# One unit of ten products per head pair, and a new order of the stages, in a two-layer decoder trunk

## The chip, the cores and the metric

The kernel runs on one core of a Trainium2 chip. The metric is the time of one execution in microseconds (us), as the device reports it. Engine names: PE is the tensor engine (matmuls), DVE the vector engine, ACT the scalar engine, POOL the GpSimd engine, SP the engine whose queue issues all the transfers (DMAs) here.

## The reference

The trunk has two residual layers over 256 positions of width 1024, in float32. Each layer normalizes its input, projects it once, runs two mixers, multiplies every mixer's output by a gate, and projects the result back. Layer 0 has a depthwise convolution and an attention over blocks (called b in the kernel). Layer 1 has an attention with three branches (c) and a sliding-window attention (d). The part that is changed is the end of the three branches:

```
kc = _rmsnorm(_compress(k_cmp, ...), kn_cmp)          # compressed keys, by a small MLP
vc = _compress(v_cmp, ...)
p_c = _masked_softmax(s_c, dist_c >= 0)
o_cmp = einsum(p_c, vc)                               # compressed branch
o_slc = ... einsum(p, selected v)                     # selected branch
o_win = _banded_attention(qg, k_win, v_win, ...)      # local branch
o = gt[0] * o_cmp + gt[1] * o_slc + gt[2] * o_win     # gates, per head and position
```

Eight query heads share two key heads, so they are worked on as four pairs.

## The kernel before, in words

Everything is computed transposed, with channels or positions on the 128 partitions. A projection is made of three float32r matmuls per piece (high by high, low by high, high by low): the weight is loaded as `raw_X`, ACT makes its high part `hi_X`, DVE or POOL the rest `lo_X`, and the input stands ready as `hhi` and `hlo`. The loads go through a ring of five `raw` buffers, the parts through nine.

The names in the rows: `pj_X` is a projection's accumulator (`kv`, `cc`, `qc`, `kd`, `qd`, `zc`, `zd` in layer 1); `ps_ht` holds transposes of the normalized input of layer 1, from which `hhi` and `hlo` come; `po` is the output projection, whose result DVE adds to `x`; `xc` is the input of the compressing MLP, of which POOL makes a part from `kv` and a part from `sw`, a copy of `kv` that a DMA has moved to other partitions; `ps_hid` is that MLP's first product, 64 matmuls on small tiles; `ps_sc` and `st` belong to the compressed branch's softmax.

An attention of a head pair goes: scores on PE (`s_c`), scores plus bias and their maximum on DVE (`sn`, `mn_c`), exponentials on ACT (`p_c`), a reciprocal on DVE (`r_c`), four scalings on POOL (`p_c<-p_c,r_c`), six transposes on PE (`pt_c`), two copies on ACT (`a_c`), the products with the values on PE (`po_c`), and the gate on DVE (`y_c`). Its stages are called `attc jb` (to the exponentials) and `pvc jb` (the rest), for pair j and branch b (0 selected, 1 local); the last attention has `attd j` and `pvd j`.

The order is not that of the code. A `Recorder` takes every instruction down, each with the stage in which it stands, and its `issue()` places them one after the other: among those that its own estimate of costs lets start, the stage that stands first in the table `ORDER` wins. It also decides whether DVE or POOL makes a `lo` part. All instructions go out through one call in `issue()`, so all rows of the profile carry its line, L384, and only the names tell them apart. Matmuls that stand under `nc.together()` are one unit: nothing is placed between them. In the kernel before, `pv()` makes such a unit of four products for each branch, and the local branch's unit has the compressed branch's two products in it as well:

```
with nc.together():
    for e in range(2): ... matmul(po[o, :S], v(0, e), a0[:, e, :], start=first, stop=False)
    for e in range(2): ... matmul(po[o, P:S], v(1, e), a1[:, e, :], start=False, stop=last)
    if more:
        for e in range(2): ... matmul(po[o, :S], *more(e), start=False, stop=True)
```

The profile counts each of these float32 products as two matmuls, so the units stand in its rows as `po_c x8` and `po_c x12`.

Of the kernel before, what the change touches and what calls it, by code (L numbers as in the profile page):

```python
# [13 lines left out]
P = 128  # L14
S = 256
# [4 lines left out]
HD = 64  # L20
# [374 lines left out]
def _landing(bus, t, nbytes):  # L395

    t = max(bus, t + 1300.0)
    for until, rate in RATES:
# [14 lines left out]
               POOL=dict(PE=135.0, ACT=100.0, DVE=60.0, POOL=96.0, SP=100.0),  # L413
               SP=dict(PE=250.0, ACT=100.0, DVE=100.0, POOL=100.0, SP=100.0))
EXTRA = dict(copy=(0.0, 20000.0), minus=(80.8, 0.0), scale=(0.0, 20000.0, 20000.0))
ORDER = ["attc 11", "attb 0", "w kv 0", "za 3", "uv", "w uv 1", "pvd 0", "w zd 1", "o1 10", "pvc 31", "pvc 11",
# [11 lines left out]
RAWS, PARTS = 5, 9  # L428
WARM = 7
SHIFT = 8  # L430
# [6 lines left out]
def tile_trunk(ctx: ExitStack, tc: tile.TileContext, i: dict, out: bass.AP):  # L437
    ctx.enter_context(tc.manual_schedule())
    nc = Recorder(tc.nc, tc)
# [8 lines left out]
    def bank(tag, bufs, name):  # L448
        return psum.tile([P, 512], F32, tag=tag, bufs=bufs, name=name)
# [296 lines left out]
        nc.copy(a1, t1[:, :2 * P].rearrange("p (e t) -> p e t", e=2))  # L746
        return a0, a1

    def pv(po, a0, a1, v, first, last, more=None):

        with nc.together():
            for e in range(2):
                o = slice(e * HD, (e + 1) * HD)
                nc.tensor.matmul(po[o, :S], v(0, e), a0[:, e, :], start=first, stop=False)
            for e in range(2):
                o = slice(e * HD, (e + 1) * HD)
                nc.tensor.matmul(po[o, P:S], v(1, e), a1[:, e, :], start=False, stop=last)
            if more:
                for e in range(2):
                    o = slice(e * HD, (e + 1) * HD)  # L760
                    nc.tensor.matmul(po[o, :S], *more(e), start=False, stop=True)
# [11 lines left out]
    w = load_w("ug", [cols_of(0, 512, 512)])  # L773
# [23 lines left out]
    w = load_w("uv", [cols_of(0, 0, 512)])  # L797
# [19 lines left out]
    w = load_w("qb", [cols_of(0, 1536, 512)])  # L817
# [3 lines left out]
    w = load_w("kb", [cols_of(0, 2048, 512)])  # L821
# [43 lines left out]
    for j in range(4):  # L865
        nc.stage(f"attb {j}")
        pt = bank("pt", 2, f"ps_qk{j}")
        for b in range(NB):
            nc.tensor.transpose(pt[:, b * P:(b + 1) * P], qn[b][:, j * P:(j + 1) * P], ident)
            nc.tensor.transpose(pt[:, S + b * P:S + (b + 1) * P], kn[b][:, j * P:(j + 1) * P], ident)  # L870
        qk = work.tile([P, 2, S], F32, tag="qk", name=f"qk{j}")
        qT, kT = qk[:, 0], qk[:, 1]
        nc.scaled(qT, pt[:, :S], q8["b_qnorm_g"][:, j:j + 1])
        nc.scaled(kT, pt[:, S:], col("b_knorm_g"))
        mn, den, pp = pair_softmax(f"b{j}", j, qT, kT, False, none_init)
        nc.stage(f"pvb {j}")
        r = work.tile([P, 4], F32, tag="r", bufs=4, name=f"r_b{j}")
        nc.vector.reciprocal(out=r, in_=den)
        for u in range(4):
            scale_p(pp[u // 2][:, u % 2, :], r[:, u:u + 1])  # L880
        a0, a1 = transposed(pp[0], pp[1], f"b{j}")
        po = bank("pt", 2, f"po_b{j}")
        pv(po, a0, a1, lambda kb, e: v0[:, kb, (2 * j + e) * HD:(2 * j + e + 1) * HD], True, True)
        gate_y(4 + j, po, z[:, 4 + j], f"b{j}")

    nc.stage("ln")
# [245 lines left out]
    for j in range(4):  # L1132
        g = j // 2
        po = bank("o", 1, f"po_c{j}")
        for br in range(2):
            nc.stage(f"attc {j}{br}")
            mn, den, pp = pair_softmax(f"c{j}{br}", j, qTn[:, j], kTn[:, g, br], False, none_init)
# [5 lines left out]
            for u in range(4):  # L1143
                scale_p(pp[u // 2][:, u % 2, :], r[:, u:u + 1])
            a0, a1 = transposed(pp[0], pp[1], f"c{j}{br}")
            pv(po, a0, a1, lambda kb, e: keep[:, 2 * kb + br, P + g * HD:P + (g + 1) * HD], br == 0, False,
               (lambda e: (vcb[:, 2 * j + e, :], ac)) if br else None)
        gate_y(j, po, z1[:, j], f"c{j}")

    for j in range(4):  # L1150
# [12 lines left out]
            scale_p(pp[u // 2][:, u % 2, :], r[:, u:u + 1])  # L1163
        a0, a1 = transposed(pp[0], pp[1], f"d{j}")
        po = bank("o", 1, f"po_d{j}")
        pv(po, a0, a1, lambda kb, e: vd[:, kb, P + g * HD:P + (g + 1) * HD], True, True)
        gate_y(4 + j, po, z1[:, 4 + j], f"d{j}")

    wo = [load_w(f"o1{n}", [i["w_out"][1][:, n * 512:(n + 1) * 512]]) for n in range(2)]
# [103 lines left out]
```

## Time and profile before

| | us |
|---|---|
| median of 3 runs (269.99 to 270.39) | 270.2 |
| profiled execution | 270.53 |
| its span (first to last instruction) | 268.5 |
| PE busy | 260.0 (97%) |
| DVE busy | 197.1 (73%) |
| ACT busy | 172.3 (64%) |
| POOL busy | 108.0 (40%) |

The profiled execution is 0.33 us above the median. Busy times are sums over instructions; matmuls overlap each other, so the share of PE says that PE is seldom without an instruction, and not how fast it works. The rest of the profile is read by its steps: which instruction followed which, at what distance, and what ended an idle time.

### The profile page before, as it was taken

The numbers are of one execution on the slowest core, as the hardware profiler recorded it, in microseconds if no ns is written. First come the engines' busy times: TensorE is split into PE (matmuls) and PEld (weight loads), VectorE is DVE, ScalarE is ACT, GpSimd is POOL, SyncE is SP. The second block draws the span as 40 slices with busy tenths as digits, with TensorE's granted clock in tenths as the row PEclk, the third lists the DMA queues.
The fourth block names the chain that finished last, engine by engine and source line by source line (L and its number), as shares of the span: only waits on it lengthen the run. The fifth ranks groups of instructions, "written<-read, shape, count | busy, mean of one in ns | idle before, by whom it ended". The sixth has DMA issues, their size and how long they took to land.

```text
span 268.5 us, 5004 instructions
## 1 busy us (share of the span) xinstructions
PE 260.0 (97%) x1693; PEld 212.4 (79%) x1693; DVE 197.1 (73%) x511; ACT 172.3 (64%) x458; POOL 108.0 (40%) x143
## 2 busy tenths in 40 slices
PE   7889999999999999999899999999999999999994
PEld 5679987878789988878679879678878987667684
DVE  1399999999999999458987213589979856765231
ACT  2267779799995656656467223688869768775300
POOL 0100019858735923202424474154991420545000
PEclk9999999999999999999999999999999999999999
DMA  6998987725763445301858827498885200000031
GB/s 198 361 386 286 354 279 279 212 101 160 236 193 121 171 147 145 89 0 40 282 158 221 231 67 250 160 343 254 273 289 149 86 4 0 2 0 1 2 117 39
DMA packets 28072, 44.89 MB, mean 167 GB/s; under 512 B 3344, under 2 KB 10256, under 8 KB 28048
## 3 DMA queue, kind: packets, MB, share of 16 engines
q1 hardware_dynamic: 28048, 44.58, 50.9%
q8 instruction: 13, 0.21, 0.3%
q14 instruction: 11, 0.09, 0.1%
HBM read 43.26 MB, written 1.05 MB: 165 GB/s over the span
## 4 chain that ended last, share of the span: by engine, by line
PE 61%; DVE 13%; DMA 12%; ACT 5%; POOL 3%; issue 3%; SPq 2%; DVEq 0%; POOLq 0%; ACTq 0%
PE po L384 15%; PE pj_zd L384 5%; PE pj_vb L384 4%; PE pj_za L384 4%; PE pj_zb L384 4%; PE pj_qc L384 4%; PE pj_kv L384 4%; DMA h<-in_prm_dram 3%; PE po_c L384 3%; DMA raw_o<-in_w_out_dram 3%; DMA raw_qd<-in_o_w_in_dram 2%; SPq L384 2%; DMA raw_kb<-in_e_w_in_dram 2%; PE pj_cc L384 2%; PE pt_c L384 2%
## 5 line engine op out<-in xcount | busy, mean ns | idle before, releaser
L384 POOL TENSOR_SCALAR p_c<-p_c,r_c 128x128 f32<-128x128 f32 (+1 forms) x32 | 19.5, 625 | 27.1 <-ACT th_zd L384 8.9
L384 DVE SCALAR_TENSOR_TENSOR acc_m<-hc,cw,acc_m 128x256 f32<-128x256 f32 x58 | 28.0, 483 | 0.2
L384 DVE SCALAR_TENSOR_TENSOR acc_o<-hc,cw,acc_o 128x256 f32<-128x256 f32 x58 | 28.1, 484 | 0.0
L384 PE MATMUL po<-hi_o,yh 128*128 128x512 f32 (+1 forms) x72 | 27.0, 382 | 0.0
L384 PE MATMUL po<-hi_o,yl 128*128 128x512 f32 (+1 forms) x72 | 27.0, 379 | 0.0
L384 PE MATMUL po<-lo_o,yh 128*128 128x512 f32 (+1 forms) x72 | 26.8, 374 | 0.0
L384 POOL TENSOR_TENSOR lo_vb<-raw_vb,hi_vb 128x1024 fp32r<-128x1024 f32 x4 | 9.5, 2409 | 25.7 <-ACT hi_vb L384 25.7
L384 ACT CAST hi_o<-raw_o 128x1024 fp32r<-128x1024 f32 x16 | 16.4, 1045 | 3.4 <-DMA raw_o<-in_w_out_dram 1.6
L384 DVE TENSOR_TENSOR lo_o<-raw_o,hi_o 128x1024 fp32r<-128x1024 f32 x13 | 15.7, 1213 | 1.5 <-ACT hi_o L384 1.5
L384 PE MATMUL pj_ug<-h,raw_ug 128*128 128x256 f32 x64 | 15.4, 392 | 1.4 <-DMA raw_ug<-in_e_w_in_dram 1.4
L384 PEld LDWEIGHTS po<-hi_o,yl 128*128 128x128 f32 x72 | 13.5, 188 | 2.9 <-issue 0.7
L384 ACT ACTIVATE p_c<-sn,mn_c 128x256 f32<-128x256 f32 (+1 forms) x32 | 14.3, 450 | 2.2 <-DVE mn_c L384 2.2
L384 PEld LDWEIGHTS po<-hi_o,yh 128*128 128x128 f32 x72 | 13.6, 189 | 2.7 <-issue 0.3
L384 PEld LDWEIGHTS pj_ug<-h,raw_ug 128*128 128x128 f32 x64 | 12.2, 197 | 3.8 <-issue 2.3
L384 PEld LDWEIGHTS po<-lo_o,yh 128*128 128x128 f32 x72 | 13.6, 188 | 1.9
L384 POOL TENSOR_TENSOR rsx<-ssx,mhalf 128x1 f32<-128x1 f32 x4 | 2.7, 680 | 27.0 <-DVE ssx L384 27.0
L384 DVE TENSOR_TENSOR x<-x,po 128x512 f32<-128x512 f32 (+1 forms) x9 | 5.6, 625 | 8.6 <-PE po L384 8.6
L384 DVE CUSTOM_DVE_ANT_0 sn<-s_c,shp 128x256 f32<-128x256 f32 (+1 forms) x32 | 10.7, 349 | 1.6 <-ACT p_c L384 0.9
L384 POOL TENSOR_TENSOR lo_o<-raw_o,hi_o 128x1024 fp32r<-128x1024 f32 x3 | 7.2, 2417 | 7.0 <-ACT hi_o L384 7.0
L384 PE MATMUL pj_zd<-hlo,hi_zd 128*128 128x256 f32 x32 | 9.4, 295 | 0.0
L384 POOL TENSOR_SCALAR p_b<-p_b,r_b 128x128 f32<-128x128 f32 (+1 forms) x16 | 8.6, 555 | 1.9 <-DVE r_b L384 1.5
L384 PE MATMUL pj_zc<-hhi,lo_zc 128*128 128x256 f32 x32 | 9.2, 287 | 0.2 <-DVE lo_zc L384 0.2
(334 smaller groups left out, 916.5 us busy)
## 6 DMA issues: line engine op xcount, KB each, us to landing
raw_o<-in_w_out_dram SPq DMA_DIRECT2D x16, 512.0 KB, 5.1
raw_uv<-in_e_w_in_dram SPq DMA_DIRECT2D x4, 512.0 KB, 8.3
raw_qb<-in_e_w_in_dram SPq DMA_DIRECT2D x4, 512.0 KB, 5.4
raw_kb<-in_e_w_in_dram SPq DMA_DIRECT2D x4, 512.0 KB, 5.8
raw_vb<-in_e_w_in_dram SPq DMA_DIRECT2D x4, 512.0 KB, 4.7
raw_zb<-in_e_w_in_dram SPq DMA_DIRECT2D x4, 512.0 KB, 4.5
raw_za<-in_e_w_in_dram SPq DMA_DIRECT2D x4, 512.0 KB, 3.6
raw_kv<-in_o_w_in_dram SPq DMA_DIRECT2D x4, 512.0 KB, 3.7
```

The lines of the kernel that those rows point to most:

```text
L384: getattr(self.real[e], method)(*args, **kw)
```

## The change

`pv()` takes a list of branches and puts all their products, and the compressed ones, under one `nc.together()`. For the three branches this makes one unit of ten products per head pair, issued in the stage `pvc j1`; the callers for b and d only pass their one branch as a list. The table `ORDER` is written anew from end to end: its entries all stand in another order, so instructions move on every engine, from the first layer on. The work is the same: 1476 matmul instructions with the same shapes.

```diff
-ORDER = ["attc 11", "attb 0", "w kv 0", "za 3", "uv", "w uv 1", "pvd 0", "w zd 1", "o1 10", "pvc 31", "pvc 11",
...
+ORDER = ["pvb 2", "w zc 1", "kd 0", "norm0 r1", "za 1", "norm0 0", "o0 01", "ln", "pvd 1", "norm0 r0", "w qc 0",
...
-    def pv(po, a0, a1, v, first, last, more=None):
-
+    def pv(po, sides, more=None):
+
+
+        n = 0
         with nc.together():
-            for e in range(2):
-                o = slice(e * HD, (e + 1) * HD)
-                nc.tensor.matmul(po[o, :S], v(0, e), a0[:, e, :], start=first, stop=False)
-            for e in range(2):
-                o = slice(e * HD, (e + 1) * HD)
-                nc.tensor.matmul(po[o, P:S], v(1, e), a1[:, e, :], start=False, stop=last)
+            for a0, a1, v in sides:
+                n += 1
+                for e in range(2):
+                    o = slice(e * HD, (e + 1) * HD)
+                    nc.tensor.matmul(po[o, :S], v(0, e), a0[:, e, :], start=n == 1, stop=False)
+                for e in range(2):
+                    o = slice(e * HD, (e + 1) * HD)
+                    nc.tensor.matmul(po[o, P:S], v(1, e), a1[:, e, :], start=False, stop=n == len(sides) and not more)
             if more:
...
         po = bank("o", 1, f"po_c{j}")
+        sides = []
         for br in range(2):
...
-            pv(po, a0, a1, lambda kb, e: keep[:, 2 * kb + br, P + g * HD:P + (g + 1) * HD], br == 0, False,
-               (lambda e: (vcb[:, 2 * j + e, :], ac)) if br else None)
+            sides.append((a0, a1, lambda kb, e, br=br: keep[:, 2 * kb + br, P + g * HD:P + (g + 1) * HD]))
+        pv(po, sides, lambda e: (vcb[:, 2 * j + e, :], ac))
         gate_y(j, po, z1[:, j], f"c{j}")
```

**The unit itself.** On PE, the products of head pair 0 before (`a0_c00` and `a1_c00` are the selected branch, `a0_c01` and `a1_c01` the local one, `vcb` the compressed one; some hundred other instructions stand where the dots are):

```order
L384 MATMUL s_c201_117_2568<-kTn_20_1764,qTn_28_2020 128x256
L384 MATMUL po_c0_97_2573<-a0_c00_202_2217,keep_21_1684 64x256 x2
L384 MATMUL po_c0_97_2573<-a1_c00_203_2235,keep_21_1684 64x128 x2
L384 MATMUL pj_zd0_86_2584<-hhi_4_186,hi_zd0_113_2317 128x256
...
L384 MATMUL pj_zd3_89_2803<-hhi_4_186,hi_zd1_115_2347 128x256
L384 MATMUL po_c0_97_2573<-a0_c01_213_2509,keep_21_1684 64x256 x2
L384 MATMUL po_c0_97_2573<-a1_c01_214_2607,keep_21_1684 64x128 x2
L384 MATMUL po_c0_97_2573<-ac_185_2680,vcb_25_2215 64x256 x2
L384 MATMUL pj_zd3_89_2803<-hlo_5_199,hi_zd1_115_2347 128x256
```

And with the change:

```order
L384 MATMUL s_c111_112_2626<-kTn_20_1753,qTn_28_2181 128x256
L384 MATMUL po_c0_97_2636<-a0_c00_202_2591,keep_21_1684 64x256 x2
L384 MATMUL po_c0_97_2636<-a1_c00_203_2619,keep_21_1684 64x128 x2
L384 MATMUL po_c0_97_2636<-a0_c01_213_2568,keep_21_1684 64x256 x2
L384 MATMUL po_c0_97_2636<-a1_c01_214_2579,keep_21_1684 64x128 x2
L384 MATMUL po_c0_97_2636<-ac_185_2438,vcb_25_2169 64x256 x2
```

The two pieces of pair 0 stand as one; the same holds for pair 3, while the pieces of pairs 1 and 2 stood next to each other already.

**The start of layer 1.** On DVE, between the output projection of layer 0 and the first projection of layer 1, before (`x1` is the residual, `lo_kv` and `lo_cc` are weight parts, `hlo` the low part of the new input):

```order
L384 TENSOR_TENSOR lo_kv2_70_1562<-raw_kv2_35_1329,hi_kv2_69_1546 128x2x512
L384 TENSOR_TENSOR lo_kv3_72_1571<-raw_kv3_36_1369,hi_kv3_71_1559 128x2x512
L384 TENSOR_TENSOR x1_2_105<-x1_2_105,po010_57_1447 128x512
L384 SCALAR_TENSOR_TENSOR hlo_5_199<-ps_ht100_60_1543,hhi_4_186 128x4x128
L384 SCALAR_TENSOR_TENSOR hlo_5_199<-ps_ht101_61_1553,hhi_4_186 128x4x128
L384 TENSOR_TENSOR x1_2_105<-x1_2_105,po011_59_1341 128x512
```

And with the change:

```order
L384 TENSOR_TENSOR lo_kv2_70_1561<-raw_kv2_35_1376,hi_kv2_69_1544 128x2x512
L384 SCALAR_TENSOR_TENSOR hlo_5_194<-ps_ht100_60_1541,hhi_4_186 128x4x128
L384 SCALAR_TENSOR_TENSOR hlo_5_194<-ps_ht101_61_1548,hhi_4_186 128x4x128
L384 TENSOR_TENSOR lo_kv3_72_1584<-raw_kv3_36_1417,hi_kv3_71_1571 128x2x512
L384 TENSOR_TENSOR lo_cc0_74_1593<-raw_cc0_37_1447,hi_cc0_73_1581 128x2x256
L384 TENSOR_TENSOR lo_cc1_76_1600<-raw_cc1_38_1487,hi_cc1_75_1589 128x2x256
L384 TENSOR_TENSOR x1_2_105<-x1_2_105,po011_59_1439 128x512
```

`hlo` has moved ahead of one `lo_kv` and of an addition to `x1`, and `lo_cc0` and `lo_cc1`, which POOL made before, stand on DVE.

**The compressing MLP.** On PE, the first of its products before, behind the last matmuls of the query projection `pj_qc`:

```order
L384 MATMUL pj_qc0_70_1852<-hi_qc3_87_1722,hhi_4_186 128x512
L384 MATMUL pj_qc0_70_1852<-lo_qc3_88_1734,hhi_4_186 128x512
L384 MATMUL pj_qc0_70_1852<-hi_qc3_87_1722,hlo_5_199 128x512
L384 MATMUL ps_hid_76_1934<-w1k0_49_1759,xc_22_1331 32x256 x2
L384 MATMUL ps_hid_76_1934<-w1v0_50_1775,xc_22_1331 32x256 x2
```

And with the change:

```order
L384 MATMUL pj_qc0_70_1851<-hi_qc1_83_1694,hhi_4_186 128x512
L384 MATMUL pj_qc0_70_1851<-lo_qc1_84_1708,hhi_4_186 128x512
L384 MATMUL ps_hid_76_1919<-w1k0_49_1759,xc_22_1303 32x256 x2
...
L384 MATMUL ps_hid_76_1919<-w1v1_52_1859,xc_22_1303 32x256 x2
L384 MATMUL pj_qc0_70_1851<-hi_qc1_83_1694,hlo_5_194 128x512
L384 MATMUL pj_qc0_70_1851<-hi_qc2_85_1710,hhi_4_186 128x512
```

The first half of the MLP's products now stands 13 matmuls ahead of the end of `pj_qc0`; the second half, one block before, has become two.

## Rows read from the trace of the kernel before

**Rows 1.** Page: busy time by engine, then the shares of the chain that ended last.

```profile
PE 260.0 (97%) x1693; PEld 212.4 (79%) x1693; DVE 197.1 (73%) x511; ACT 172.3 (64%) x458; POOL 108.0 (40%) x143
PE 61%; DVE 13%; DMA 12%; ACT 5%; POOL 3%; issue 3%; SPq 2%; DVEq 0%; POOLq 0%; ACTq 0%
```

**Rows 2.** The chain that ended last, in order of time: start, us, engine and group.

```profile
204.31 0.80 PE po_c L384 x8
...
212.94 0.86 PE s_c L384 x8
...
218.83 1.23 PE po_c L384 x12
...
221.87 1.88 PE po_c L384 x20
```

**Rows 3.** Timeline of PE, into the unit at 218.76: start, us, engine, instruction.

```profile
218.43 0.28 PE L384 MATMUL pj_zd<-hhi,lo_zd 128*128 128x256 f32 x1
218.55 0.28 PE L384 MATMUL pj_zd<-hhi,hi_zd 128*128 128x256 f32 x1
218.76 0.87 PE L384 MATMUL po_c<-a_c,keep 128*64 128x256 f32 x8
```

**Rows 4.** Timeline, all engines, at layer 1's start (in brackets idle time and releaser).

```profile
124.16 4.59 DVE L384 TENSOR_TENSOR lo_kv<-raw_kv,hi_kv 128x1024 fp32r<-128x1024 f32 x3
...
126.25 3.65 POOL L384 TENSOR_TENSOR lo_cc<-raw_cc,hi_cc 128x512 fp32r<-128x512 f32 x2 [3.45 <-ACT hi_cc L384]
...
128.67 0.68 DVE L384 TENSOR_TENSOR x<-x,po 128x512 f32<-128x512 f32 x1
128.82 0.39 PE L384 MATMUL pj_kv<-lo_kv,hhi 128*128 128x512 f32 x1
129.27 1.28 DVE L384 SCALAR_TENSOR_TENSOR hlo<-ps_ht,hhi 128x512 fp32r<-128x512 f32 x2
...
130.00 0.50 PE L384 MATMUL pj_kv<-hi_kv,hlo 128*128 128x512 f32 x1 [0.80 <-DVE hlo L384]
...
130.34 0.40 PE L384 MATMUL pj_kv<-hi_kv,hhi 128*128 128x512 f32 x1
130.57 0.39 PE L384 MATMUL pj_kv<-lo_kv,hhi 128*128 128x512 f32 x1
```

**Rows 5.** Page: DVE's splits of 128x1024 (count, busy, mean ns, idle before).

```profile
L384 DVE TENSOR_TENSOR lo_o<-raw_o,hi_o 128x1024 fp32r<-128x1024 f32 x13 | 15.7, 1213 | 1.5 <-ACT hi_o L384 1.5
```

**Rows 6.** Timeline, all engines, around the MLP's input and its first products.

```profile
148.95 0.37 ACT L384 COPY kv<-pj_cc 128x256 f32<-128x256 f32 x1
...
154.69 3.45 POOL L384 TENSOR_TENSOR xc<-sw,prm 64x120 f32<-64x120 f32 x8 [3.25 <-DMA sw<-kv]
...
159.99 0.41 PE L384 MATMUL ps_hid<-w1k,xc 128*32 128x256 f32 x2
```

**Rows 7.** DMA issues, 146 to 162 us: KB each, median us to landing.

```profile
w1k<-in_c_k_w_dram SPq DMA_DIRECT2D x4, 256.0 KB, 4.2
...
sw<-kv SPq DMA_DIRECT2D x2, 128.0 KB, 4.3
```

**Rows 8.** Timeline of PE, two more waits.

```profile
189.20 0.28 PE L384 MATMUL pj_zc<-hlo,hi_zc 128*128 128x256 f32 x1
189.64 0.39 PE L384 MATMUL pj_zc<-hhi,lo_zc 128*128 128x256 f32 x1 [0.16 <-DVE lo_zc L384]
...
198.42 0.33 PE L384 MATMUL pt_c<-ident,p_c 128*128 128x128 f32 x1
199.30 0.33 PE L384 MATMUL ps_sc<-ident,st 128*128 128x128 f32 x1 [0.55 <-ACT st L384]
```

**Rows 9.** Timeline, DVE and POOL at once in layer 0.

```profile
63.36 0.48 DVE L384 SCALAR_TENSOR_TENSOR acc_m<-hc,cw,acc_m 128x256 f32<-128x256 f32 x1
63.43 2.41 POOL L384 TENSOR_TENSOR lo_zb<-raw_zb,hi_zb 128x1024 fp32r<-128x1024 f32 x1
63.75 0.48 DVE L384 SCALAR_TENSOR_TENSOR acc_o<-hc,cw,acc_o 128x256 f32<-128x256 f32 x1
```

**Rows 10.** Timeline of POOL: scalings of one head pair in layer 0, and in layer 1.

```profile
71.51 0.84 POOL L384 TENSOR_SCALAR p_b<-p_b,r_b 128x128 f32<-128x128 f32 x2 [0.42 <-PE s_b L384]
...
217.01 1.62 POOL L384 TENSOR_SCALAR p_c<-p_c,r_c 128x128 f32<-128x128 f32 x4 [3.26 <-DVE r_c L384]
```

More of the change, by code (lines that the diff above doesn't have):

```diff
@@ L882, in tile_trunk @@
         po = bank("pt", 2, f"po_b{j}")
-        pv(po, a0, a1, lambda kb, e: v0[:, kb, (2 * j + e) * HD:(2 * j + e + 1) * HD], True, True)
+        pv(po, [(a0, a1, lambda kb, e: v0[:, kb, (2 * j + e) * HD:(2 * j + e + 1) * HD])])
         gate_y(4 + j, po, z[:, 4 + j], f"b{j}")
@@ L1165, in tile_trunk @@
         po = bank("o", 1, f"po_d{j}")
-        pv(po, a0, a1, lambda kb, e: vd[:, kb, P + g * HD:P + (g + 1) * HD], True, True)
+        pv(po, [(a0, a1, lambda kb, e: vd[:, kb, P + g * HD:P + (g + 1) * HD])])
         gate_y(4 + j, po, z1[:, 4 + j], f"d{j}")
```

22 rows, old and new, of the table ORDER are left out of this document.

## The prediction, made before the changed kernel ran

> **What bounds the kernel now.** I read the busy times first, then the chain of work that ended last, then PE's timeline wherever two matmuls stand farther apart than their kind usually does. PE is busy 260.0 of 268.5 us and makes up 61% of the chain [rows 1], so the time is PE's list of instructions, plus the places where PE finds its next operand not ready. A change that does the same matmuls can gain in two ways only: cheaper neighbours on PE, or fewer waits. After the loads of the first 57 us I find these waits that are worth anything: 0.95 us at the start of layer 1 [rows 4], 0.3 us at 189.6 and 0.76 us at 199.3 [rows 8]; some others are 0.1 to 0.2 us each. From 200 us to the end there is none, and PE runs through its order as fast as it goes.
>
> **The sum is made against** the profiled execution, 270.53 us, which is 0.33 above the median of 270.2; I take the difference over as it is.
>
> **The unit of ten.** The view of the chain prices the pieces: a unit of 8 takes 0.80 us, one of 12 takes 1.23, and the two next to each other (x20) 1.88 [rows 2]. Joining saves 0.80 + 1.23 - 1.88 = 0.15 us. Entering the unit costs too: the step from a matmul on the whole array into the unit is 0.21 us, where two of the same kind are 0.12 apart [rows 3]; a joined pair enters once less, 0.09 us. But two of the four pairs stood next to each other before, so only pairs 0 and 3 gain: 2 x (0.15 + 0.09) = 0.48 us. The MLP's products, one block more than before, take back an entry, which no row prices apart; by the one above it is 0.09. Elsewhere the new order has some tile shapes in better and some in worse company; between 0 and 0.2 gained, of which I take 0.1. Together **-0.5**, bounds -0.7 and -0.3. So what the words of the change say is a fifth of a per cent, and the table of the order decides.
>
> **The start of layer 1.** PE's second `pj_kv` matmul starts at 128.82, the third at 130.00; at a step of 0.23 (130.34 to 130.57) that is 0.95 lost, and the restart step of 0.34 loses another 0.11 [rows 4]. It waits for `hlo`, which DVE does last: three `lo_kv` in 4.59 us, then an addition to `x` (0.68), then `hlo` (1.28) [rows 4]. A split of that size takes 1.21 us alone [rows 5], so three would be 3.6; the 0.96 beyond that fell while POOL made `lo_cc` for 3.65 us [rows 4]. In the new order `hlo` follows the third `lo_kv` at once, POOL makes no `lo_cc` there, and between the transposes that `hlo` is made from and `pj_kv` stand 21 matmuls of the output projection, 21 x 0.23 = 4.8 us of cover against at most 1.21 + 1.28 of DVE work. The wait goes: **-1.06**, bounds 0 (if the transposes themselves come late) and -1.06. What is late next is the second half of the input: after its addition to `x` DVE now has a `lo_cc` to do ahead of the normalization, half of a 1.21 split, while PE comes to those transposes after the same 20 matmuls, without the 1.06 of standing still. I take **+0.15**, bounds 0 and 0.5.
>
> **The MLP's products.** Here the new order makes a wait. `xc` must be complete: ACT copies `kv` (148.95), two DMAs move it, and POOL's eight writes from `sw` end at 154.69 + 3.45 = 158.14 [rows 6]. Before, PE came to `ps_hid` at 159.99 and waited for nothing. Now the first half stands 13 matmuls of `pj_qc` earlier, 13 x 0.23 = 3.0 us, so PE would come at 157.0 on the old clock. An earlier start of layer 1 does not help, because `kv` follows `pj_cc` on PE and moves with it. PE stands still from 157.0 to 158.2: **+1.2**. Behind the waiting matmul are the rest of `pj_qc`, its norm on POOL, and all scores of the attention. Bounds: nothing, if the copies land in 3.1 us instead of 4.3; and 2.5, if they land no sooner than before although layer 1 starts 1.3 us sooner, since they share the queues with the MLP's weights, which take 4.2 [rows 7].
>
> **The two later waits.** `lo_zc` at 189.6 (0.44 for a step of 0.12) and `st` at 199.3 (0.88 for 0.12) cost 0.32 + 0.76 = 1.08 [rows 8]. In the new order the third quarter of the MLP's products comes before the last attention's key projection and the last one right behind it (both stood behind it before), so their weight buffers come free earlier, SP issues the loads of `qd` and `zc` earlier, and the compressed softmax starts earlier against the scores that cover it. By adding up the steps in the new order I find both ready 0.4 us or more before PE asks: **-1.05**, bounds 0 and -1.08.
>
> **Layer 0.** Both orders ask DVE for the same convolution at 0.39 us per step [rows 9], with the softmax between. From 57 us on DVE has no gap, so I add up its list: in the new order the reciprocal for head pair 2 comes at 84.3 us. The first scaling on POOL needs 0.42 more [rows 10], with the hand-overs 0.85 in all, so the transposes can start at 85.1; PE's list brings them at 84.5. The cover is thin and my sum of 70 small steps may be 0.3 off: **+0.3**, bounds 0 and 0.7. The 0.15 us waits of before, there and at `pj_qd`, are about made up by others.
>
> **Layer 1's attention.** The heads are packed closer. The tightest is the local branch of pair 1: its transposes stand 4.85 us behind its scores. A unit of before, scores at 212.94 [rows 2], had its first scaled tile about 0.4 after POOL's start at 217.01 [rows 10], 4.5 us later. So 0.3 to 0.4 us remain here, and 0.7 at the two next tightest. I take **+0.1**, bounds 0 and 1. The products are no cover that is lost: transposes and `pj_zd` stand in their place. The end is a run of `po` as before.
>
> **The sum.** -0.5 - 1.06 + 0.15 + 1.2 - 1.05 + 0.3 + 0.1 = -0.86, so 269.67 for such an execution, and 0.33 less, **269.35**, for the median.
>
> [...] DVE went on at 0.39 us per step while POOL did a `lo_zb` for 2.41 us, both of them reading two operands [rows 9]. In the new order POOL does `lo_za` 2 and 3 as well, which DVE had, two more of 2.41 in the stretch where DVE has no gap; by rows 9 that costs DVE nothing, and it frees 2 x 1.21. [...]
>
> **The rivals.**
> 1. *The waits cancel.* The direct gain of 0.5 stays, `pj_kv` gains its 1.06, and `ps_hid`, the second half of the input and layer 0 take it all back, while the softmax chains still end where they did: -0.5 - 1.06 + 0.5 + 1.2 + 0.3 - 0.5 (half of the two later waits) = -0.06, **270.1**. For it: the gains and the new waits are of one size, and each is a sum of small steps.
> 2. *No wait at `ps_hid`.* The copies land in about 3 us, when fewer weights are ahead of them: 1.2 more gained, **268.2**. Against it: the 4.3 of rows 7.
> 3. *The softmax becomes the bound (slower).* From 203 to 230 us the new order has seven units of scores, each with sums, exponentials, reciprocal and four scalings. If ACT's copies and casts fall between, a unit takes about 0.4 longer than PE's list allows: 7 x 0.4 = 2.8, less the 0.1 counted, **272.0**. For it: margins of 0.3 to 0.7 and POOL's four scalings of 1.62 in a row [rows 10]. Against: three of the seven are tight, the others have 6 us and more. It decides the sign from 0.2 us per unit on.
> 4. *DVE stops beside POOL (slower).* If `lo_za` 2 and 3 each hold DVE up as `lo_cc` seems to have done, 0.96 in 3.65 [rows 4], DVE is 4.82 x 0.26 = 1.3 late at the transposes of pair 2; if it stops altogether, 4.8. Nearer the row than the full stop, 2 us: **271.35**. It decides the sign from 1.4 on.
>
> **How the numbers follow.** Within 0.2%, 0.54 us to either side of 270.2, a measurement of this kernel can't tell a gain or a loss from no change. I give the forecast 0.5, with a range of its own of 268.7 to 270.0 from the bounds of its terms, so 0.4 of it lies below 269.66 and 0.1 within; rival 1 0.18, all within; rival 2 0.12, faster; rival 3 0.13 and rival 4 0.07, slower. That is faster 0.52, no change 0.28, slower 0.20. From 268.2 (rival 2) to 271.2, short of rival 3's full price, the range leaves out some 0.17.
>
> **What would show it.** Right: the four pieces `po_c` x20, each about 1.88; no wait of `pj_kv` for `hlo`; `ps_hid` starting with a wait of about 1.2 for POOL's `xc`; nothing before `ps_sc`; a small wait of the transposes of pair 2 in layer 0 for POOL's `p_b`. Wrong: a `ps_hid` that waits for nothing, or 2 us and more; waits of `pt_c` for POOL between 203 and 230 us that add up to over 1 us; accumulations of DVE in layer 0 farther apart than 0.39; or a new wait of PE for a load, which I expect nowhere.

## The result, and the profile after

The changed kernel takes 271.71 us (median of 19 runs, 270.8 to 273.35), the kernel before 269.99 beside it (19 runs, 269.05 to 271.17). The ratio is 1.007, 95% interval 1.0055 to 1.0086: **slower by 0.7%, 1.7 us**, where 269.35 and "faster" had been forecast. The profiled execution took 271.23 us.

The page of the kernel after answers to [rows 1]:

```profile
PE 259.4 (96%) x1693; PEld 212.5 (79%) x1693; DVE 193.6 (72%) x507; ACT 171.2 (64%) x458; POOL 108.6 (40%) x147
PE 78%; POOL 6%; DMA 6%; issue 3%; ACT 3%; SPq 2%; DVE 1%; POOLq 0%
```

PE is busy 0.6 us less and yet the span is 0.9 longer: the time is in PE's waits. From its list of waits after (what waited for what: us, times, longest), those behind the first loads that the kernel before does not have:

```profile
PE ps_kd L384 <- DVE qn_kd L384: 1.7, 1, 1.7
...
PE ps_kcT L384 <- DVE kcd L384: 0.3, 1, 0.3
PE ps_hidT L384 <- ACT hid L384: 0.3, 1, 0.3
PE pj_kd L384 <- ACT qn_qc L384: 0.2, 1, 0.2
```

The prediction has no word of the first. `ps_kd` are transposes of `qn_kd`, the last attention's normalized key: POOL makes its scale `rs_kd`, DVE multiplies. In the kernel before the views of the two tiles read (ns: shortest, median, longest):

```profile
L384 DVE TENSOR_TENSOR qn_kd<-keep,rs_kd x2: 418/421/424, 167.2 to 172.6; 128x256 f32<-128x256 f32 x2
...
L384 DVE TENSOR_TENSOR lo_qd<-raw_qd,hi_qd x4: 1206/1212/1226, 171.4 to 181.6; 128x1024 fp32r<-128x1024 f32 x4
```

The timeline there with the change:

```profile
170.67 0.42 DVE L384 TENSOR_TENSOR qn_kd<-keep,rs_kd 128x256 f32<-128x256 f32 x1 [0.27 <-POOL rs_kd L384]
...
171.23 0.70 POOL L384 TENSOR_TENSOR rs_kd<-ms_kd,mhalf 128x2 f32<-128x2 f32 x1
...
171.89 2.37 POOL L384 TENSOR_TENSOR lo_qd<-raw_qd,hi_qd 128x1024 fp32r<-128x1024 f32 x1
...
171.96 2.58 DVE L384 TENSOR_TENSOR qn_kd<-keep,rs_kd 128x256 f32<-128x256 f32 x1 [0.50 <-POOL rs_kd L384]
...
172.59 0.39 PE L384 MATMUL pj_qd<-hi_qd,hhi 128*128 128x512 f32 x1
...
174.69 0.41 PE L384 MATMUL ps_kd<-ident,qn_kd 128*128 128x128 f32 x2 [1.70 <-DVE qn_kd L384]
```

The first `qn_kd` takes DVE 0.42 us, the second 2.58, and it ends just behind POOL's `lo_qd`, which began 0.07 us ahead of it. In the kernel before DVE made all four parts `lo_qd`; the new order gives the third, `lo_qd2`, to POOL. PE stands still for 1.70 us; measured from start to start (172.59 to 174.69), the step is 1.86 longer than such steps are otherwise.

The rest came as described. At the start of layer 1, against [rows 4]:

```profile
123.66 1.22 DVE L384 TENSOR_TENSOR lo_kv<-raw_kv,hi_kv 128x1024 fp32r<-128x1024 f32 x1
124.79 1.28 DVE L384 SCALAR_TENSOR_TENSOR hlo<-ps_ht,hhi 128x512 fp32r<-128x512 f32 x2
126.16 1.23 DVE L384 TENSOR_TENSOR lo_kv<-raw_kv,hi_kv 128x1024 fp32r<-128x1024 f32 x1
...
128.59 0.39 PE L384 MATMUL pj_kv<-hi_kv,hhi 128*128 128x512 f32 x1
...
128.83 0.39 PE L384 MATMUL pj_kv<-lo_kv,hhi 128*128 128x512 f32 x1
...
129.06 0.40 PE L384 MATMUL pj_kv<-hi_kv,hlo 128*128 128x512 f32 x1
```

`hlo` is ready at 126.07, 3.0 us before PE asks for it at 129.06, and the 0.95 us wait is gone. All four units stand in the chain as one piece (start, us), as the last of [rows 2]:

```profile
209.03 1.88 PE po_c L384 x20
216.65 1.88 PE po_c L384 x20
227.21 1.88 PE po_c L384 x20
233.68 1.88 PE po_c L384 x20
```

At `ps_hid`, against [rows 6, 7], the view of the tile `sw`:

```profile
L384 POOL TENSOR_TENSOR xc<-sw,prm x8: 438/450/456, 152.2 to 155.2; 64x120 f32<-64x120 f32 x8
...
  PEld ps_hid L384: 0.4, 1
...
DMA to landing us min/median/max: 3.1/3.1/3.1
```

The copies landed after 3.1 us this time, not 4.3, and PE's weight load (PEld, a row of its own in the profile) waited 0.4 us, of which 0.11 reached the matmuls.

Aligned by instruction, from PE's 277th matmul on (behind the first loads), PE in the kernel after is 0.27 us ahead when layer 1's `pj_kv` begins, 1.56 ahead 20 matmuls later, 1.61 ahead in `pj_qc`, and 0.91 behind at its end. So 2.5 us are lost behind `pj_qc`. (The first loads took 0.28 longer in this execution and the end behind PE's last matmul 0.31 less; the two cancel.)

### The profile page after: what moved, and what is told of

Read it like the earlier page. It is cut to its first block, busy times and chain, and to the rows that moved or that the text cites. A ratio compares the mean times of both kernels' runs of the same rounds, so it can differ in the third digit from the quotient of the medians.

```text
span 269.4 us, 5006 instructions
## 1 busy us (share of the span) xinstructions
PE 259.4 (96%) x1693; PEld 212.5 (79%) x1693; DVE 193.6 (72%) x507; ACT 171.2 (64%) x458; POOL 108.6 (40%) x147
## 3 DMA queue, kind: packets, MB, share of 16 engines
HBM read 43.26 MB, written 1.05 MB: 164 GB/s over the span
## 4 chain that ended last, share of the span: by engine, by line
PE 78%; POOL 6%; DMA 6%; issue 3%; ACT 3%; SPq 2%; DVE 1%; POOLq 0%
PE po L384 17%; PE pj_zd L384 4%; PE pj_zc L384 4%; PE pj_zb L384 4%; PE pj_uv L384 4%; PE pj_vb L384 4%; PE pj_za L384 4%; PE pj_kv L384 4%; DMA h<-in_prm_dram 3%; PE pj_qc L384 3%; PE po_c L384 3%; PE pj_ug L384 3%; DMA raw_qd<-in_o_w_in_dram 2%; POOL lo_vb L384 2%; PE pt_c L384 2%
## 5 line engine op out<-in xcount | busy, mean ns | idle before, releaser
L384 PE MATMUL po<-hi_o,yl 128*128 128x512 f32 (+1 forms) x72 | 26.3, 372 | 0.0
L384 POOL TENSOR_SCALAR p_c<-p_c,r_c 128x128 f32<-128x128 f32 (+1 forms) x32 | 15.7, 509 | 18.6 <-DVE r_c L384 8.2
L384 DVE TENSOR_REDUCE ss_qc<-sq_qc 128x8 f32<-128x512 f32 x2 | 1.4, 686 | 12.5 <-ACT sq_qc L384 12.5
L384 POOL TENSOR_SCALAR p_b<-p_b,r_b 128x128 f32<-128x128 f32 (+1 forms) x16 | 7.8, 510 | 5.8 <-DVE r_b L384 5.8
L384 POOL TENSOR_SCALAR p_d<-p_d,r_d 128x128 f32<-128x128 f32 (+1 forms) x16 | 6.6, 429 | 8.5 <-ACT yh L384 4.4
L384 PE MATMUL pj_zd<-hhi,lo_zd 128*128 128x256 f32 x32 | 9.7, 304 | 0.0
```

The costliest lines, as they stand in the source:

```text
L384: getattr(self.real[e], method)(*args, **kw)
```

## The experiments

Theory A, an assumption from that one pair (2.58 us for 0.42, beside POOL's 2.37): an instruction of DVE that reads two operands in SBUF and one of POOL that reads SBUF do not run side by side; the one that starts second stands still until the first is done. The rivals are in the expectations. Except for the place of the convolution's sums, edits work on the finished order in `issue()`: `find` gives the place of an engine's nth instruction that writes a tile, `move` shifts it, `on` gives it to another engine, `later` moves matmuls past so many of `pj_qd`. Times are medians; the kernel before took 269.7 to 270.2 beside them.

**1. `lo_qd2` back on DVE.**

```diff
+k = find("POOL", "lo_qd2")
+on(k, "DVE")
+move(k, find("DVE", "qn_kd1"))
```

> The changed kernel with one instruction on another engine: the split that makes lo_qd2 (128x1024) is done by DVE, just ahead of qn_kd1, instead of by POOL. Theory A (DVE's qn_kd1 took 2.58 us instead of some 0.43 because POOL's lo_qd2 started 0.07 us before it and DVE stood still until that ended): PE's wait for qn_kd1 at 172.6, 1.86 us, shrinks to under 0.5, since DVE now has 1.21 more to do but an idle 0.5 to do it in; the time falls by 1.2 to 1.8 us against the changed kernel, to about 270.2. Theory B (the whole chain from the MLP to the compressed scores is late in the new order, and qn_kd1 is only its first link): PE waits as long at the next links, ps_kcv and ps_kcT, and the time falls by less than 0.5 us.

270.27 us, ratio to before 1.0012 (0.9988 to 1.0035): 1.44 us less than the changed kernel, by moving one instruction. DVE's timeline:

```profile
171.65 1.22 DVE L398 TENSOR_TENSOR lo_qd<-raw_qd,hi_qd 128x1024 fp32r<-128x1024 f32 x1
172.79 0.42 DVE L398 TENSOR_TENSOR qn_kd<-keep,rs_kd 128x256 f32<-128x256 f32 x1
```

DVE does 1.22 us more work ahead of `qn_kd`, and `qn_kd` is yet done 1.1 us after its `rs_kd`, instead of 2.6.

**2. Another form of the multiplication**, with `lo_qd2` still on POOL.

```diff
-tensor_tensor(qn_kd1, keep, rs_kd1, op=mult)
+scalar_tensor_tensor(qn_kd1[:, h], in0=keep[:, h], scalar=1.0, in1=rs_kd1[:, h], op0=mult, op1=mult)   # h = 0, 1
```

> The changed kernel with lo_qd2 still on POOL and every instruction in its place, but qn_kd1 is computed by two SCALAR_TENSOR_TENSOR instructions (one for each head, the same product with a factor of 1) instead of one TENSOR_TENSOR. Theory A in its narrow form (POOL stops a TENSOR_TENSOR on DVE, not a SCALAR_TENSOR_TENSOR, as the accumulations of layer 0 went on at 0.39 us beside POOL's splits): the two take 0.3 us each, PE's wait falls by 1.5 us and more, and the time by 1.5 to 2. Theory A in its wide form (any DVE instruction with two operands in SBUF is stopped): the first of the two takes 2.4 us and nothing is gained. Theory B: under 0.5 us.

271.11 us, ratio 1.0052 (1.0034 to 1.007): 0.6 less than the changed kernel, with intervals that overlap.

```profile
171.57 2.36 POOL L398 TENSOR_TENSOR lo_qd<-raw_qd,hi_qd 128x1024 fp32r<-128x1024 f32 x1
171.63 2.65 DVE L398 SCALAR_TENSOR_TENSOR qn_kd<-keep,rs_kd 128x128 f32<-128x128 f32 x2
```

The other form stands still as well, 2.65 us for the two; what it shares with the TENSOR_TENSOR is that both operands lie in SBUF. This is the form of the convolution's accumulations in [rows 9], which did not stop; their second operand is the sum, and that lies in PSUM. In the two profiles of before and after, 186 of those accumulations overlapped an instruction of POOL by more than 0.1 us, and they took 0.45 to 0.49 us, like the ones that overlapped none (0.47 to 0.49).

**3. A pause on POOL.** A memset of 64 columns ahead of POOL's `lo_qd2`, nothing else.

```diff
+order.insert(find("POOL", "lo_qd2"), ("POOL", "memset", pad, 0.0))
```

> The changed kernel with one instruction more: a memset of 64 columns on POOL between rs_kd1 and lo_qd2, so that DVE's qn_kd1 starts ahead of POOL's split and not 0.07 us behind it. Theory A says that the later one of the two is held: qn_kd1 takes some 0.43 us instead of 2.58, and POOL's split is held for about 0.4 instead. What that is worth: PE needs lo_qd2 itself three matmuls behind the transposes of qn_kd1, and POOL ends it at about 174.7; so theory A with this second wait expects PE to wait 1.0 to 1.4 us for lo_qd2 instead of 1.86 for qn_kd1, and the time to fall by 0.3 to 0.8. If the order of start does not matter (the two are slow whenever they overlap), qn_kd1 still takes over 2 us and nothing is gained.

270.54 us, ratio 1.0026 (1.0005 to 1.0048): one more instruction, 1.2 us less, where 0.3 to 0.8 had been expected.

```profile
172.02 0.15 POOL L397 MEMSET pad<- 128x64 f32 x1
...
172.10 0.43 DVE L397 TENSOR_TENSOR qn_kd<-keep,rs_kd 128x256 f32<-128x256 f32 x1
172.13 2.65 POOL L397 TENSOR_TENSOR lo_qd<-raw_qd,hi_qd 128x1024 fp32r<-128x1024 f32 x1
...
174.83 0.50 PE L397 MATMUL pj_qd<-lo_qd,hhi 128*128 128x512 f32 x1 [0.53 <-POOL lo_qd L397]
```

Now DVE starts first and POOL stands still for 0.3 us. Which of the two starts first decides, and 0.07 us had decided it; without the memset POOL starts first in the profiles of experiment 6 and of the first kernel of experiment 9 as well, and `qn_kd` takes 2.58 us in both. PE then waits 0.53 us for `lo_qd`, so this is no full cure.

**4. The convolution's sums in SBUF.** The step of the prediction itself, tested: `acc_m` and `acc_o` take the place of `ya` in SBUF.

```diff
-acc_m, acc_o = two banks of PSUM
+acc_m, acc_o = ya[:, 0:2], ya[:, 2:4]
```

> The changed kernel, with one thing else: the sums of layer 0's convolution, which DVE keeps in PSUM (acc_m, acc_o), are kept in SBUF, in the place of the result ya. Each accumulation then reads two operands in SBUF instead of one. Same instructions in the same order. Theory A (the later starter stands still as long as the other engine's instruction lasts, if the DVE instruction has two operands in SBUF): beside the POOL instructions of layer 0 single accumulations take 2 us and more instead of 0.48, or the POOL instructions (lo_zb, lo_za 2.4 us, scalings 0.4) are the ones that stretch; DVE has no gap there, so PE waits for DVE or POOL and the kernel becomes slower by 2 to 10 us. My reading of rows 9 in the prediction (two operands in SBUF run beside POOL unhindered): accumulations stay at 0.39 us per step, time within 0.5 us of the changed kernel.

305.08 us, ratio 1.1286 (1.1235 to 1.1337): **35 us slower**, where 2 to 10 had been expected. POOL's timeline and then DVE's:

```profile
57.49 5.31 POOL L391 TENSOR_SCALAR ms_kb<-ss_kb 128x8 f32<-128x8 f32 x1 [3.50 <-ACT sq_kb L391]
...
65.73 12.61 POOL L391 TENSOR_TENSOR lo_zb<-raw_zb,hi_zb 128x1024 fp32r<-128x1024 f32 x1
```

```profile
64.18 11.97 DVE L391 SCALAR_TENSOR_TENSOR ya<-hc,cw,ya 128x256 f32<-128x256 f32 x30
```

POOL's `ms_kb` takes 5.31 us instead of 0.20 and a `lo_zb` 12.61 instead of 2.41. The `lo_zb` starts during the fourth of DVE's 30 accumulations, which stand one behind the other, and it ends 2.2 us behind the last one: it is held by the whole rest of the row. So DVE's instructions in [rows 9] did not meet theory A's condition, two operands in SBUF, and those rows spoke neither for it nor against it.

Not all of the 35 us is standing still. The page's row of PE's granted clock (40 slices of 7.6 us, in tenths of full speed, 9 for 90% or more):

```profile
PEclk9999999967789799799999999999999999999999
```

In single slices between 61 and 129 us, in layer 0, where PE newly waits (12.7 us at `ps_qk`), the granted clock was in the 0.6s to 0.8s; the changed kernel has 1.00 there. PE is busy 269.8 us for the same 1693 matmuls, 10.4 more than in the changed kernel. The edit also moves the sums' writes to SBUF; but DVE's `z`, which are made from one operand in SBUF and one in PSUM and written to SBUF, took 0.39 to 0.42 us beside POOL in the profiles of before and after, and 0.36 to 0.42 alone, so it is the reading that counts.

**5. `lo_cc` on DVE in the kernel before**, behind `hlo`.

```diff
+on(find("POOL", "lo_cc0"), "DVE"), on(find("POOL", "lo_cc1"), "DVE")   # both moved behind hlo
```

> The kernel before with two instructions moved: lo_cc0 and lo_cc1 on DVE, behind hlo, instead of on POOL beside DVE's third lo_kv. Theory A: the third lo_kv takes 1.21 us instead of some 2.3, hlo ends 1.1 us sooner and PE's wait of 0.95 at 130.0 is gone or nearly so; the second half of the input comes up to 0.5 later; the time falls by 0.5 to 1.0 us against the kernel before. Theory B says nothing of this place; if the wait at 130.0 is due to the order on DVE alone (x ahead of hlo), the third lo_kv stays at 2.3 and the time is the same.

269.98 us, ratio 1.0007 (0.9991 to 1.0022): the 0.5 to 1.0 us that had been expected are not there. DVE's timeline, against [rows 4], and PE at the next transposes:

```profile
123.47 3.49 DVE L400 TENSOR_TENSOR lo_kv<-raw_kv,hi_kv 128x1024 fp32r<-128x1024 f32 x3
...
133.91 0.63 PE L400 MATMUL ps_ht<-ident,ht 128*128 128x128 f32 x4 [1.22 <-DVE ht L400]
```

Without `lo_cc` on POOL three `lo_kv` take 3.49 us, not 4.59, and the wait for `hlo` goes; DVE is then late at `ht`, and PE waits 1.22 us there. The changed kernel has `lo_cc` on DVE too and keeps its gain; what it has besides is another order of DVE's list.

**6. The units apart again**, in the new order: those of pairs 0, 2 and 3 split behind four products, two projection matmuls between.

```diff
-po_c: 10 products in one unit
+po_c: 4 products, two matmuls of pj_zd or po, 6 products
```

> The changed kernel with the unit of ten taken apart again in three of the four pairs (0, 2 and 3): the selected branch's four products, then two float32r matmuls of a projection that stood shortly ahead of the unit, then the other six. Same work, all else in place. My pricing: 0.15 us for the missing neighbour and 0.09 for the second entry, so 0.24 per pair: PE's rows show about 2.0 to 2.1 us for x8 and x12 where x20 was 1.88, and the time rises by 0.5 to 0.9 us against the changed kernel. [...]

273.93 us, ratio 1.0145 (1.0115 to 1.0175). The chain of waits, first unit:

```profile
209.10 0.80 PE po_c L411 x8
210.34 1.23 PE po_c L411 x12
```

From the first split unit to the last PE loses 1.9 us against the changed kernel: 0.35 at the first, and 0.63 a pair on the average, where the prediction priced a pair at 0.24. The average holds more than the units: the two matmuls were taken from other places, and the steps there changed as well. The rest of the 2.2 us stands elsewhere.

**7. The unit alone, in the order of before**: the first pieces of pairs 0 and 3 moved down to the second.

```diff
+for j in (0, 3): move(first piece of po_c{j}, second piece of po_c{j})   # with tiles of their own for a0_c{j}0, a1_c{j}0
```

> The kernel before in its old order, with the unit of ten alone: for pairs 0 and 3 the first four products are moved down to stand right ahead of the other six (the tiles that they read get a place of their own meanwhile, so that nothing else has to wait). By the prediction's term the two pairs gain 0.48 us. By the run that took the units apart, where a pair was worth 0.35 by the unit's own rows and 0.63 by the whole stretch, they gain 0.7 to 1.3 us: 268.7 to 269.3. Rival: the neighbours in the old order take it back, time within 0.3 us of before.

270.68 us, ratio 1.0038 (1.002 to 1.0056): **slower by 0.9 us.** PE's list of waits:

```profile
PE pt_c L409 <- POOL p_c L409: 0.6, 1, 0.6
...
PE pt_c L409 <- ACT a_c L409: 0.4, 1, 0.4
```

PE's timeline where pair 3's first piece stood, in the kernel before and in this one:

```profile
231.82 0.50 PE L384 MATMUL po<-hi_o,yl 128*128 128x512 f32 x1
232.26 0.87 PE L384 MATMUL po_c<-a_c,keep 128*64 128x256 f32 x8
...
233.63 0.39 PE L384 MATMUL po<-hi_o,yl 128*128 128x512 f32 x1
```

```profile
231.86 0.50 PE L409 MATMUL po<-hi_o,yl 128*128 128x512 f32 x1
...
232.66 0.40 PE L409 MATMUL po<-hi_o,yl 128*128 128x512 f32 x1
```

The stretch takes 1.81 us with the piece and 0.80 without: 1.0 us given back here, and 0.80 at pair 0 by the same measure. Where the pieces stand now, each unit takes 1.88 instead of 1.23, 0.65 more. So pair 0 gains 0.15 and pair 3 gains 0.35, together 0.50, as much as the prediction's 0.48, though not in equal parts. Pair 0's first piece had stood behind `s_c`, small tiles too, and the first step among the `pj_zd` that follow is 0.23 us with and without it (205.04 to 205.27, and 203.71 to 203.94), where the next ones are 0.12; pair 3's had stood between two `po`.

Against that, two steps into transposes became 0.51 and 0.73 us longer: the pieces had been the work that covered a copy of ACT for pair 1 and POOL's scalings for pair 3. The change as its words put it, alone, makes this kernel slower.

**8. The other waits of the changed kernel mended.** The chain from the MLP goes over `hid`, its transposes `hidT`, `hx`, the second product `kcv`, the compressed keys `kcn` and `kcd`, their transposes `kcT`, the compressed scores `st` and the softmax `sc`. First, `lo_qd2` on DVE behind the eighth `hx`, and `hi_qd2` on ACT behind `hid` (run twice; the profile is the second run's):

```diff
+move(find("ACT", "hi_qd2"), find("ACT", "hid") + 1)
+k = find("POOL", "lo_qd2"); on(k, "DVE"); move(k, find("DVE", "hx", 7) + 1)
```

> The changed kernel with ACT's hi_qd2 behind the copy of hid, and lo_qd2 on DVE behind the hx that feed the second MLP product. Theory A: PE's waits at ps_hidT (0.45) and ps_kd1 (1.86) are both gone, lo_qd2 itself may come up to 0.5 late; the time falls by 1.8 to 2.5 us against the changed kernel, to 269.2 to 269.9, at or below the kernel before. Theory B: the waits move to ps_kcv, ps_kcT and ps_sc0, and less than 0.8 us is gained.

> The kernel of e5 once more, for a profile of an undisturbed execution: hi_qd2 behind the copy of hid on ACT, lo_qd2 on DVE behind the hx. Theory A: qn_kd1 takes 0.43 us; the waits at ps_hidT and ps_kd1 are under 0.2 us each; PE may wait up to 0.5 for lo_qd2; the time is 1.8 us under that of the changed kernel, within 0.3 of the kernel before. Theory B: 1.5 us of waits in all at ps_kcv, ps_kcT and ps_sc0.

269.85 and 270.04 us, ratios 0.9993 (0.9969 to 1.0017) and 0.9997 (0.9971 to 1.0024): the time of the kernel before. Then five moves, and three more:

```diff
+k = find("POOL", "lo_qd2"); on(k, "DVE"); move(k, find("DVE", "qn_kd0") + 1)   # hi_qd2 as above
+later("ps_kd0", 2); later("ps_kd1", 4); later("ps_kcv", 2)
+move(find("DVE", "lo_qd3"), find("DVE", "kcn"))
+# three more: hi_qd3 behind the first keep, qTn ahead of hi_zc0, kcd ahead of lo_zc0
```

> The changed kernel with five moves around the key and query projections of layer 1, aimed at the waits that its trace shows: ACT makes hi_qd2 behind the copy of hid, DVE makes lo_qd2 right behind the first qn_kd (POOL has it no more), the two transposes of the first kd block stand two matmuls later and those of the second four later, lo_qd3 stands ahead of kcn, and the second products of the MLP stand two matmuls later. Theory A: DVE's qn_kd takes 0.43 us, and of the waits for qn_kd (1.86), hidT (0.45) and, by a gap between DVE's instructions in which POOL's ms_kc can start, kcT (0.41), most go: 2.2 to 2.8 us less than the changed kernel, 268.7 to 269.4, faster than the kernel before by 0.3 to 0.5%. If the gain of taking lo_qd2 away has nothing to do with what runs beside it, these moves give no more than the 1.7 us that two of them gave: 269.9 to 270.1.

> The kernel of the run before (the changed kernel with five moves) with three more, aimed at the two waits that its trace still shows behind them (0.31 us at s_c, 0.51 at ps_kcT): ACT makes hi_qd3 right behind the first keep, so that lo_qd3 no longer holds kcn up on DVE; the two copies qTn stand ahead of hi_zc0; kcd stands ahead of lo_zc0. Theory: PE waits there for the last of a chain over DVE, ACT and POOL, and both waits go: 0.5 to 0.8 us less, 269.0 to 269.3, 0.2 to 0.3% faster than the kernel before. Rival: the chain has only been pushed along, a wait of the same size shows at the compressed scores or at the gate projections (pj_zc): 269.8.

269.77 and 269.85 us, ratios 0.9998 (0.9977 to 1.002) and 0.9997 (0.9973 to 1.002): both times near the rival's time and not at the forecast, 268.7 to 269.4. The second rival's reason is the one that shows: waits came back farther down the chain, at `s_c` and `ps_kcT` (0.2 and 0.4), then at `ps_kcv` and `ps_st` (0.2 and 0.4). The first rival's reason, that it does not matter what runs beside `lo_qd2`, does not follow from the time: both `qn_kd` take 0.42 us here.

**9. The wait that had been predicted.** In the kernel with two edits of experiment 8 the view of `sw` reads:

```profile
  PEld ps_hid L399: 1.2, 4
...
DMA to landing us min/median/max: 3.8/3.9/4.0
```

Up to there it is the same program as the changed kernel. In eight profiles with `ps_hid` in this place (those of the changed kernel and of experiments 1 to 3, 6 and 8) the copies land after 3.1 to 4.1 us, and the first 32 matmuls of `ps_hid` take 1.97 to 3.06 us, against 1.86 before: 0.11 to 1.20 lost, 0.78 in the middle. So the first half was moved down 13 matmuls, to where it stood before, in the changed kernel, in that of eight moves, and in that of experiment 1:

```diff
+for n in (1, 0): move(find("PE", "ps_hid", n), find("PE", "pj_qc0", 23) + 1)
```

> The changed kernel with one thing else: the first half of the MLP's products (ps_hid, 32 matmuls) stands behind the last of pj_qc's first 24 matmuls, as in the kernel before, 13 matmuls later than in the changed one. In the six profiled kernels of the new order PE's weight load for ps_hid waited 0.4 to 1.2 us in all for xc, the more the later the copies sw landed (3.1 to 4.3 us after their issue). Theory: the wait that the prediction put there (+1.2, bounds 0 to 2.5) is there, and goes: 0.4 to 1.2 us less than the changed kernel, 270.4 to 271.2. Rival: the wait for qn_kd behind it takes it all, since that chain hangs on POOL and DVE: within 0.3 us of the changed kernel.

> The changed kernel with the eight moves of the run before and ps_hid moved back 13 matmuls. In that run's profile PE's weight load waited 0.9 us for xc in ps_hid. Theory: ps_hid waits for nothing and the gain reaches the end: 0.5 to 1.2 us less than 269.85, that is 268.7 to 269.3, 0.2 to 0.4% faster than the kernel before. Rival: the chain from the MLP to the compressed softmax starts later by as much, and PE waits at ps_st instead: 269.8.

> The changed kernel with two edits: DVE makes lo_qd2 just ahead of the second qn_kd, and ps_hid stands 13 matmuls later. The first alone gave 270.27, 1.45 us less than the changed kernel, with a wait of 0.65 us at ps_hid in its profile. Theory: 0.4 to 0.9 us less, 269.4 to 269.9, the same as the kernel before or just below. Rival: what PE gains at ps_hid it waits at hidT and kcT: 270.2.

273.67, 272.16 and 272.16 us, ratios 1.0141 (1.0105 to 1.0177), 1.0078 (1.0047 to 1.0108) and 1.0093 (1.0057 to 1.0129): 2 us slower than their partners, against both theories. The waits of weight loads in the first:

```profile
PEld ps_hid L397 <- DMA w1v<-in_c_v_w_dram: 2.7, 2, 2.1
```

The weights `w1` go through the ring of five `raw` buffers, and the third quarter's last load can only start when the first quarter's products have freed theirs. Next, four matmuls instead of thirteen, in the kernel of experiment 1 and in that of eight moves; then, in the latter, all of the MLP where it stood before:

```diff
+for n in (1, 0): move(find("PE", "ps_hid", n), find("PE", "pj_qc0", 14) + 1)   # 14: four later; 23: thirteen
+move(find("PE", "ps_hid", 2), find("PE", "ps_hid", 3))                          # in the third kernel alone
```

> The changed kernel with lo_qd2 on DVE ahead of the second qn_kd (270.27 alone), and the first half of ps_hid four matmuls later instead of thirteen: 4 x 0.23 = 0.92 us of work for PE in the place of a wait of 0.4 to 1.2 us for xc. The half then ends hardly later than now, so the weight buffers that it frees are not delayed, as they were by thirteen matmuls, where PE waited 2.7 us for w1v. Theory (the wait for xc takes part of the gain): 0.4 to 0.9 us less, 269.4 to 269.9. Rival (the chain behind the MLP decides, wherever PE waits for it): 270.2.

> The same four matmuls in the kernel with eight moves (269.85, with a wait of 0.9 us for xc and one of 0.47 at ps_st in its profile). Theory: 269.0 to 269.4, 0.2 to 0.3% faster than the kernel before. Rival: 269.8, and the wait at ps_st grows to about 1.2.

> The kernel with eight moves and with all of ps_hid where the kernel before has it: the first half behind pj_qc, the rest in one block ahead of pj_qd. No weight load is then asked for early: no wait of ps_hid for w1v (2.6 us in the run with the first half alone moved) and none for xc. Theory that the early MLP only cost waits: 269.0 to 269.5. Rival (it was bought with them: the weights of the last projections come later, as in the kernel before): waits for lo_zc and at ps_sc as in rows 8 return, 1 us or more, 270 to 271.

270.8, 270.29 and 273.69 us, ratios 1.005 (1.0024 to 1.0076), 1.0015 (0.9996 to 1.0033) and 1.0157 (1.0127 to 1.0187). None is faster than its partner. In the third PE waits 3.4 us at the first `pj_qd`, whose first weights ACT can take up at 169.45 instead of 166.03. So the early MLP of the new order costs the wait at `ps_hid` and lets the loads behind it start early; moving it gained nothing.

## Why the prediction was wrong, step by step

- **The step that failed is the one on DVE beside POOL's `lo_zb`**, and with it the sum, which puts what POOL gets anew at no cost for DVE. It read [rows 9] as DVE running unhindered beside POOL with "both of them reading two operands". The sums of those rows are in PSUM, so DVE read one operand in SBUF. Experiments 1 to 4 agree with theory A: beside POOL's `lo_qd2` DVE's instructions with both operands in SBUF took 2.58 and 2.65 us, the accumulations with one in PSUM 0.45 to 0.49 beside POOL's instructions in layer 0. Read rightly, rows 9 spoke neither way, and the three `lo_kv` of [rows 4] spoke for theory A: 4.59 us beside `lo_cc`, 3.49 without it (experiment 5). By theory A, each pair of a POOL instruction and a DVE instruction with two SBUF operands that the new order brings together had to be looked for; the prediction looked at `lo_za` alone, whose neighbours read PSUM, and not at `lo_qd2`. What the runs showed in its place: beside it `qn_kd` takes 2.58 us instead of 0.42 and PE loses 1.86. Rival 4 had the mechanism, with a chance of 0.07, but in layer 0; that its 271.35 is near the 271.71 is luck.
- **The sum**, -0.86 forecast and +0.70 measured for the profiled execution (0.33 off 269.67 is 269.34; the 269.35 is a slip of 0.01). The wait for `qn_kd`, 1.86, is more than the 1.56 between them. In the medians, 269.35 against 271.71, taking `lo_qd2` from POOL gives 1.44 of 2.36 back (experiment 1); the other 0.9 is not separated. Smaller new waits, not forecast, are `hidT` 0.45, `ps_kcT` 0.41 (behind POOL's `ms_kc`, 2.59 us for 32x1 elements beside three such instructions of DVE) and three of 0.2.
- **The unit**, -0.5: the size was right. Joining the two pairs gave 0.50 in the old order (experiment 7), and if every step between two neighbours on PE is put at the mean of its kind, without the longest and the shortest tenth, the new order's list adds up to 0.56 less than the old one's (0.71 by medians). "The products are no cover that is lost" held for the new order; in the old one the lost cover cost more than the joining gave.
- **The start of layer 1**, -1.06 + 0.15: right, -1.29 over those 20 matmuls and no loss at the second half.
- **`ps_hid`**, +1.2: the wait exists, for the reason given, with 0.11 in this profile and up to 1.20 in others. What it lacked was that the landing time of `sw` differs from one execution to the next: 4.3 us in rows 7, 3.2 and 3.3 in two other profiles of the old order. "Wrong: a `ps_hid` that waits for nothing" was nearly what the matmul rows alone showed; the weight loads had to be read as well.
- **The two later waits**, -1.05: right, 0.32 and 0.76 went; 0.2 came back at `ps_sc`.
- **Layer 0**, +0.3: wrong, -0.27; no transposes waited. **Attention**, +0.1: right, PE waits for no scaling between 203 and 230 us, so rival 3 did not happen.

What stays open: with `lo_qd2` on DVE all mended versions stop at the time of before, though the start of layer 1 gains 1.3 us. The profiles of experiment 8 show 1.0 to 1.2 us lost at `ps_hid`, and small waits along the MLP's chain. The moves of experiments 8 and 9 point to that chain and the loads as what bounds the stretch, but how much each takes was not separated, and no version beat the kernel before.

## What to carry to other kernels

When a reordering moves an elementwise instruction between DVE and POOL, list its new neighbours on the other engine and where each operand lies; where DVE read two operands in SBUF and POOL read SBUF at the same time in these runs, the one that started second stood still until the other was done (DVE 2.58 us for 0.42, POOL 12.61 for 2.41), and 0.07 us of order decided which one that was. A row that seems to contradict a theory must meet the theory's condition before it counts. And before pieces of PE work are joined, ask what each piece covers where it stands: that cover is lost with the move.

## What the runs showed that had not been expected

POOL did not get in between DVE instructions that stood back to back: held by one of 30, it waited for all that were left, 12.61 us for an instruction of 2.41. A memset of 0.15 us, which only writes, made a kernel 1.2 us faster by letting DVE start first. The same 128 KB copies between partitions landed after 3.1 to 4.7 us in profiles of programs that are the same up to these copies.
